# Four instead of five groups of projections for the resting tokens, and an earlier start of two sparse jobs

## The chip, the cores and the metric

The kernel runs on one core of a Trainium2 chip. The metric is the device time of one execution in microseconds, given as the median over several runs.

## The reference

Two layers of a transformer trunk over 256 tokens of width 1024. In each layer one product with a wide matrix gives all projections at once; three kinds of attention work on them, and gates merge their outputs:

```python
fq, fk, fv, ff, sq, sk, sv, dq, dk, dv, iq, ik, iw, g = split_cols(x @ w_in)
# widths:   384 384 384 6  320 320 320  320 64 64  512 64 8  3072
o_fox = fox_attention(fq, fk, fv, log_sigmoid(ff))          # 6 heads, softmax with decay
o_sb  = stick_breaking_attention(sq, sk, sv)                # 5 heads
o_dsa = dsa_attention(rope(dq), rope(dk), dv, rope(iq), rope(ik), iw)   # 5 heads, one k and v
merged = sum(sigmoid(g_i) * (o_i @ w_up_i))
x = layer_norm(alpha * x + merged @ w_out)
x = layer_norm(alpha * x + squared_relu(x @ w_ff_in) @ w_ff_out + gated embedding)
```

(Written here in short; batch, biases and blocks are left out.) The sparse attention (dsa) has an indexer: eight heads of scores `relu(iq . ik)`, weighted with `iw` and summed, pick the 64 keys of a query that its softmax may see. Each head has 64 columns.

## The kernel before

Every float32 value that enters a matmul is held as a high part (a cast by ACT, line 159) and a low part (DVE's subtraction, line 160), made by `split`; a product is three matmuls, high by high, high by low and low by high (`mm3`, line 174). Weights come in units through five buffers each for the raw load (`wr`, line 106), the high part (`wh`) and the low part (`wl`).

The projections are made in two ways. In `xstat` the tokens rest in TensorE and the weights' columns move: a group of up to 512 columns takes two PSUM banks (`pg`, of which there are four in turn), one per tile of 128 tokens, and goes through the eight blocks of 128 inputs in four units of two. A unit is 12 matmuls, six for each token tile, a group 48. Its output has tokens on the partitions, as the values, the gates and the projections that are rotated (`do_rope`, lines 497 to 501 on DVE and an addition on POOL, lines 504 and 506) want it. In `wstat` the weights rest and 256 tokens move; the queries and keys of the fox heads (`fox`, 768 columns, three banks) and of the stick-breaking heads (`sb`, 640 columns, three banks, lines 557 to 560) come that way. When a group ends, its `done` reads the banks; a bank is free for the next group when its last reader is through.

The order is written by hand. `PRODUCTS` names the groups in turn: fv, fox, iq1, iq2, dsa, sb, sv, and then the gates g1 to g5 of 512 columns each. `JOBS` names the attention jobs in turn, each with the number of steps to wait before the next may start: fox0, fox2, fox4 and sb0, sb2, sb4 are pairs of heads (sb4 is the fifth stick-breaking head alone), idxT, idx0 and idx1 the indexer, dsaT transposes, and dsa0, dsa1 and dsa3 sparse heads (one, two and two). The main loop goes by steps. In each step every job in flight goes on to its next yield, the next job starts if its projections are made and the wait is over, and units of projections are issued until 550 columns are reached. After the last unit come at most two units of the up-projections (`up`, 12 matmuls of 512 columns) as filling. Behind the loop, ACT makes the sigmoids of the gates (line 1043, after a load of another function table), and the up-projections go on with sigmoids between them.

A pair of softmax heads goes: scores on TensorE (line 181) into two banks `ps` of four; a reduction with the mask on DVE (line 771), exponentials on ACT (line 774), a reciprocal and a scale on DVE (lines 776 and 779); three transposes per head on TensorE (line 194); the split of the transposed probabilities `t3k` (ACT line 159, DVE line 160); the values, six matmuls (line 174). A stick-breaking job has its own sums (lines 878 to 882), additions (884 and 885), exponential (886), a mask on POOL (841), cast (889) and low part (890) before its values.

Of the kernel before, what the change touches and what calls it, by code (L numbers as in the profile page):

```python
# [10 lines left out]
F32 = mybir.dt.float32  # L11
# [19 lines left out]
PRODUCTS = ['fv', 'fox', 'iq1', 'iq2', 'dsa', 'sb', 'sv', 'g1', 'g2', 'g3', 'g4', 'g5']  # L31
JOBS = [('decay', 4), ('fox0', 2), ('fox2', 2), ('fox4', 1), ('idxT', 1), ('idx0', 3), ('idx1', 0), ('dsaT', 2), ('sb0', 2), ('sb2', 2), ('dsa0', 0), ('sb4', 2), ('dsa1', 1), ('dsa3', 4)]
# [20 lines left out]
def hybrid_trunk(ctx, tc, x, p, w_in, b_forget, w_up_fox, w_up_sb, w_up_dsa, w_out,  # L53
# [29 lines left out]
    def rope_parts(nh):  # L83

        if nh == 1:
            ab = act.tile([P, 2 * HD], F32, tag="t05", name=nm("t05"), bufs=2)
            return [ab[:, i * HD:(i + 1) * HD].rearrange("p (h d) -> p h d", d=HD) for i in range(2)]
        return [t15(F32)[:, :nh * HD].rearrange("p (h d) -> p h d", d=HD) for _ in range(2)]
# [22 lines left out]
    def wrows(w, l, k0, nk, c0, n):  # L111
        return [(ALLP, w[l, k0 * P:(k0 + nk) * P, c0:c0 + n].rearrange("(k p) n -> p k n", p=P))]
# [376 lines left out]
    for l in range(L):  # L489
# [3 lines left out]
        def do_rope(t, src, nh, dst, dup=1):  # L493

            s3 = src.rearrange("p (h d) -> p h d", d=HD)
            a, b = rope_parts(nh)
# [6 lines left out]
            if dup == 1:  # L503
                nc.gpsimd.tensor_add(dst.rearrange("p (h d) -> p h d", d=HD), a, b)
            else:
                nc.gpsimd.tensor_add(dst.rearrange("p (h d) -> p h d", d=HD),
                                     a.to_broadcast([P, dup, HD]), b.to_broadcast([P, dup, HD]))
# [127 lines left out]
        def idx_T():  # L635
            q = ps()
            for t in range(2):
                nc.tensor.transpose(q[:, t * P:(t + 1) * P], rnk[t][:, 0:128], ident)
# [71 lines left out]
        def dsa_T():  # L710
            q = ps()
            for t in range(2):
                nc.tensor.transpose(q[:, t * P:(t + 1) * P], rnk[t][:, 128:256], ident)
# [266 lines left out]
        def chain(*gs):  # L980
# [15 lines left out]
        jobs = {"decay": (("fv",), lambda: decay()), "idxT": (("iq1", "iq2"), idx_T),  # L996
                "idx0": (("iq1", "iq2"), lambda: idx_scores(0)),
                "idx1": (("iq1", "iq2"), lambda: idx_scores(1)),
                "dsaT": (("dsa", "sv"), dsa_T)}
# [229 lines left out]
```

## Time and profile before

| | |
|---|---|
| median of 3 runs | 863.86 us (863.65 to 865.48) |
| the profiled execution | 863.92 us, span 862.2 us, granted clock 0.998 |
| TensorE busy | 850.3 us, 99%, 4691 matmuls |
| DVE busy | 641.5 us, 74%, 1143 instructions |
| ACT busy | 471.3 us, 55%, 753 instructions |
| POOL busy | 65.8 us, 8% |
| DMA | 154.46 MB, 179 GB/s |

The profile's span begins with the first instruction; 1.7 us of the execution's time lie around it. A timeline row gives the start, the busy time of the row's instructions together, engine, line, operation, output and inputs, and in square brackets the idle time before it and who ended it. Matmuls overlap, so that the time of one is read from start to start. The rows below are of layer 1; layer 2 follows in the second half of the span.

### The profile page before, as it was taken

The numbers are of one execution on the slowest core, as the hardware profiler recorded it, in microseconds if no ns is written. First come the engines' busy times: TensorE is split into PE (matmuls) and PEld (weight loads), VectorE is DVE, ScalarE is ACT, GpSimd is POOL, SyncE is SP. The second block draws the span as 40 slices with busy tenths as digits, with TensorE's granted clock in tenths as the row PEclk, the third lists the DMA queues.
The fourth block names the chain that finished last, engine by engine and source line by source line (L and its number), as shares of the span: only waits on it lengthen the run. The fifth ranks groups of instructions, "written<-read, shape, count | busy, mean of one in ns | idle before, by whom it ended". The sixth has DMA issues, their size and how long they took to land.

```text
span 862.2 us, 12952 instructions
## 1 busy us (share of the span) xinstructions
PE 850.3 (99%) x4691; PEld 732.9 (85%) x4691; DVE 641.5 (74%) x1143; ACT 471.3 (55%) x753; POOL 65.8 (8%) x136
## 2 busy tenths in 40 slices
PE   9999999999999999999999999999999999999996
PEld 7999988878888888888889998888788888888885
DVE  5679997779867666666866899967898776666666
ACT  5556657694455454444545566667834544444440
POOL 1012010100011000000100211001001100000100
PEclk9999999999999999999999999999999999999999
DMA  8754665626666666666645557555274766666741
GB/s 265 226 145 132 204 194 171 169 76 205 206 221 190 192 188 193 192 192 205 210 128 156 145 162 226 155 169 171 89 232 153 233 192 187 189 193 194 232 134 50
DMA packets 80385, 154.46 MB, mean 179 GB/s; under 512 B 10305, under 2 KB 26049, under 8 KB 80321
## 3 DMA queue, kind: packets, MB, share of 16 engines
q1 hardware_dynamic: 78720, 149.17, 56.0%
q0 software_dynamic: 1600, 4.46, 1.8%
q8 instruction: 37, 0.61, 0.3%
q14 instruction: 28, 0.22, 0.1%
HBM read 152.30 MB, written 1.05 MB: 178 GB/s over the span
## 4 chain that ended last, share of the span: by engine, by line
PE 85%; issue 6%; DVE 4%; ACT 3%; DMA 1%; POOL 0%; DVEq 0%; SPq 0%; POOLq 0%
PE pg L174 46%; PE ps L1112 14%; PE ps L1116 7%; PE pg L239 4%; PE ps L181 2%; PE pg L557 2%; PE pg L246 2%; PE pg L559 2%; PE pg L560 2%; PE ps L194 1%; DVE wl L160 1%; PE ps L174 1%; PE pg L373 1%; ACT t2k L1043 1%; DMA wr<-in_w_in_dram 1%
## 5 line engine op out<-in xcount | busy, mean ns | idle before, releaser
L160 DVE TENSOR_TENSOR wl<-wr,wh 128x1024 fp32r<-128x1024 f32 (+4 forms) x295 | 333.6, 1143 | 160.1 <-ACT wh L159 157.7
L159 ACT CAST wh<-wr 128x1024 fp32r<-128x1024 f32 (+4 forms) x295 | 288.3, 984 | 286.7 <-PE pg L174 99.8
L174 PE MATMUL pg<-wh,t16k 128*128 128x512 f32 (+4 forms) x784 | 227.6, 365 | 0.1
L174 PE MATMUL pg<-wh,t2k 128*128 128x512 f32 x528 | 165.9, 390 | 0.0
L174 PEld LDWEIGHTS pg<-wh,t16k 128*128 128x128 f32 x784 | 142.9, 188 | 20.7 <-DVE t2k L167 0.7
L174 PE MATMUL pg<-wl,t16k 128*128 128x512 f32 (+4 forms) x392 | 142.0, 362 | 0.0
L1112 PE MATMUL ps<-t16k,wh 128*128 128x512 f32 x512 | 127.8, 391 | 0.0
L174 PEld LDWEIGHTS pg<-wh,t2k 128*128 128x128 f32 x528 | 99.2, 188 | 20.3
L1112 PEld LDWEIGHTS ps<-t16k,wh 128*128 128x128 f32 x512 | 93.1, 189 | 17.3
L174 PE MATMUL pg<-wl,t2k 128*128 128x512 f32 x264 | 102.9, 390 | 0.0
L174 PEld LDWEIGHTS pg<-wl,t16k 128*128 128x128 f32 x392 | 73.7, 188 | 8.5 <-DVE wl L160 0.2
L1116 PEld LDWEIGHTS ps<-t16k,wl 128*128 128x128 f32 x512 | 69.8, 190 | 5.0
L1116 PE MATMUL ps<-t16k,wl 128*128 128x256 f32 x512 | 71.4, 282 | 0.0
L174 PEld LDWEIGHTS pg<-wl,t2k 128*128 128x128 f32 x264 | 49.6, 188 | 9.7
L557 PE MATMUL pg<-t16k,wh 128*128 128x256 f32 x176 | 50.5, 287 | 0.4 <-DVE t16k L160 0.4
L560 PE MATMUL pg<-t16k,wl 128*128 128x256 f32 x176 | 49.8, 283 | 0.0
L559 PE MATMUL pg<-t16k,wh 128*128 128x256 f32 x176 | 49.7, 283 | 0.0
L174 PE MATMUL pg<-wh,t1k 128*128 128x512 f32 x112 | 37.4, 398 | 0.0
L557 PEld LDWEIGHTS pg<-t16k,wh 128*128 128x128 f32 x176 | 33.6, 191 | 0.9 <-issue 0.8
L559 PEld LDWEIGHTS pg<-t16k,wh 128*128 128x128 f32 x176 | 33.7, 191 | 0.0
L560 PEld LDWEIGHTS pg<-t16k,wl 128*128 128x128 f32 x176 | 33.7, 191 | 0.0
L774 ACT ACTIVATE t3k<-t3k,small 128x128 f32<-128x128 f32 (+1 forms) x44 | 19.7, 449 | 14.7 <-DVE small L771 14.7
(211 smaller groups left out, 1002.1 us busy)
## 6 DMA issues: line engine op xcount, KB each, us to landing
wr<-in_w_ff_in_dram SPq DMA_DIRECT2D x64, 512.0 KB, 4.3
wr<-in_w_ff_out_dram SPq DMA_DIRECT2D x64, 512.0 KB, 4.0
wr<-in_w_in_dram SPq DMA_DIRECT2D x46, 512.0 KB, 4.3
wr<-in_w_in_dram SPq DMA_DIRECT2D x32, 384.0 KB, 3.8
wr<-in_w_out_dram SPq DMA_DIRECT2D x16, 512.0 KB, 3.8
wr<-in_w_ple_gate_dram SPq DMA_DIRECT2D x16, 512.0 KB, 4.4
wr<-in_w_in_dram SPq DMA_DIRECT2D x16, 256.0 KB, 3.2
wr<-in_w_in_dram SPq DMA_DIRECT2D x8, 390.0 KB, 4.2
```

What stands on the lines that cost most here:

```text
L159: a = nc.scalar.copy(hi, src)
L160: b = nc.vector.tensor_sub(lo, src, hi.bitcast(F32))
L174: nc.tensor.matmul(o, l, r, start=start and i == 0, stop=stop and i == 2, skip_group_check=skip)
L181: nc.tensor.matmul(o, a[i == 2], b[i == 1], start=start and i == 0, stop=stop and i == 2)
L239: nc.tensor.matmul(o[t][:, :n], tok(aT, u * nk + kk, t)[0], wt[i][kk], start=u + kk + i == 0, stop=False)
L246: nc.tensor.matmul(o[t][:, :n], tok(aT, kb, t)[1], units[kb // nk][0][kb % nk], start=False, stop=kb == nkb - 1)
L557: nc.tensor.matmul(oi, hi, rh, start=kb == 0 and i % 2 == 0, stop=False, skip_group_check=True)
L559: nc.tensor.matmul(oi, hi, rl, start=False, stop=False, skip_group_check=True)
L560: nc.tensor.matmul(oi, lo, rh, start=False, stop=kb == KB - 1, skip_group_check=True)
L774: nc.scalar.activation(pr[:, i, sl], pr[:, i, sl], AF.Exp, bias=mn[:, t:t + 1], scale=-1.0, accum_out=mn[:, 2 + t:3 + t])
L1112: nc.tensor.matmul(pz[i], wt[0][:, kk, i * P:(i + 1) * P], x1_both[:, 2 * u + kk, :], start=u + kk == 0, stop=False, skip_group_check=True)
L1116: nc.tensor.matmul(pz[i][:, 0:T], wt[1][:, kk, i * P:(i + 1) * P], x1T[0][:, 2 * u + kk, :], start=False, stop=2 * u + kk == KB - 1, skip_ ...
```

## The change

The 1742 columns that go through `xstat` are cut anew. Before: fv 390, iq1 320, iq2 264, dsa 384, sv 384. Now: fv 390, iq 512 (all eight indexer queries), ix 392 (three sparse query heads, the sparse key and value, the indexer key and weights; loaded by two transfers a unit, of 320 and of 72 columns), sv 448 (the stick-breaking values and the first two sparse query heads). The ropes follow: iq two of four heads, ix one of two heads (both keys, each written twice) and one of three, sv one of two. In `JOBS` the step between sb4 and dsa1 goes from 2 to 1.

With a group fewer, the steps that issue projections go from 28 to 26 a layer. Counted from the last of them, dsa1 and dsa3 start one unit of 12 matmuls earlier, sb0, sb2 and dsa0 one unit later. The number of loads of weights in these groups is 16 a layer before and now. `PE` has 4691 matmuls before, and 48 a layer fewer now.

The core of the diff:

```diff
-PRODUCTS = ['fv', 'fox', 'iq1', 'iq2', 'dsa', 'sb', 'sv', 'g1', 'g2', 'g3', 'g4', 'g5']
-JOBS = [('decay', 4), ('fox0', 2), ('fox2', 2), ('fox4', 1), ('idxT', 1), ('idx0', 3), ('idx1', 0), ('dsaT', 2), ('sb0', 2), ('sb2', 2), ('dsa0', 0), ('sb4', 2), ('dsa1', 1), ('dsa3', 4)]
+PRODUCTS = ['fv', 'fox', 'iq', 'ix', 'sb', 'sv', 'g1', 'g2', 'g3', 'g4', 'g5']
+JOBS = [('decay', 4), ('fox0', 2), ('fox2', 2), ('fox4', 1), ('idxT', 1), ('idx0', 3), ('idx1', 0), ('dsaT', 2), ('sb0', 2), ('sb2', 2), ('dsa0', 0), ('sb4', 1), ('dsa1', 1), ('dsa3', 4)]
...
-        def c2_done(t, o):
-            do_rope(t, o[:, 192:256], 1, rnk[t][:, 0:128], dup=2)
-            nc.vector.tensor_copy(iw[t], o[:, 256:264])
-            do_rope(t, o[:, 0:192], 3, rnq[t][:, 320:512])
-
-        def c1_done(t, o):
-            do_rope(t, o[:, 0:320], 5, rnq[t][:, 0:320])
+        def iq_done(t, o):
+            for c in (0, 256):
+                do_rope(t, heads(o[:, c:c + 256]), 4, heads(rnq[t][:, c:c + 256]))
...
-        def c4_done(t, o):
-            split(o[:, 320:384], vh[:, t, 768:832], vl[:, t, 768:832])
-            do_rope(t, o[:, 256:320], 1, rnk[t][:, 128:256], dup=2)
-            do_rope(t, o[:, 0:256], 4, rnd[t][:, 64:320])
-            nc.gpsimd.tensor_copy(rnd[t][:, 320:384], rnk[t][:, 128:192])
+        def ix_done(t, o):
+
+            split(o[:, 256:320], vh[:, t, 768:832], vl[:, t, 768:832])
+
+            do_rope(t, o[:, 192:448].rearrange("p (h c) -> p h c", c=2 * HD)[:, :, 0:HD], 2,
+                    rnk[t].rearrange("p (h c) -> p h c", c=2 * HD), dup=2)
+            nc.vector.tensor_copy(iw[t], o[:, 384:392])
+            do_rope(t, heads(o[:, 0:192]), 3, heads(rnd[t][:, 128:320]))
+            nc.gpsimd.tensor_copy(rnd[t][:, 320:384], rnk[t][:, 0:64])
             for v in (vh, vl):
                 nc.gpsimd.tensor_copy(v[:, t, 832:896], v[:, t, 768:832])
 
-        def c3_done(t, o):
+        def sv_done(t, o):
             split(o[:, 0:320], vh[:, t, 384:704], vl[:, t, 384:704])
-            do_rope(t, o[:, 320:384], 1, rnd[t][:, 0:64])
+            do_rope(t, heads(o[:, 320:448]), 2, heads(rnd[t][:, 0:128]))
...
-            "iq2": (KB, 264, lambda: xstat(xT, w_in, l, O_IQ + 320, 264, c2_done)),
-            "iq1": (KB, 320, lambda: xstat(xT, w_in, l, O_IQ, 320, c1_done)),
-            "dsa": (KB, 384, lambda: xstat(xT, w_in, l, O_DQ + 64, 384, c4_done)),
-            "sv": (KB, 384, lambda: xstat(xT, w_in, l, O_SV, 384, c3_done)),
+            "iq": (KB, 512, lambda: xstat(xT, w_in, l, O_IQ, 512, iq_done)),
+            "ix": (KB, 392, lambda: xstat(xT, w_in, l, [(O_DQ + 128, 320), (O_IK, 72)], 392, ix_done)),
+            "sv": (KB, 448, lambda: xstat(xT, w_in, l, O_SV, 448, sv_done)),
```

The rest of the diff lets `wrows` take a list of column ranges, lets `do_rope` write a head twice for two heads at once, and changes the names in the jobs' conditions. Behind the changed lines the line numbers are eight to eleven higher.

The order on the engines changes at three places that matter below. First, DVE where the first stick-breaking unit waits for a bank, in layer 1. `ps_1038` and `ps_1039` are the score banks of a pair of fox heads (`mfox` is their mask), `pg_948` is the bank of the first token tile of the group dsa. Before:

```order
L771 ISA t3k_1037,small_1145<-ps_1039,mfox 128x256
L771 ISA small_1145 128x1
L776 RECIPROCAL small_1056<-small_1056 128x2
L160 TENSOR_TENSOR t16k_288<-pg_948,t16k_288 128x64
L779 TENSOR_SCALAR t3k_1037<-t3k_1037,small_1056 128x128
L779 TENSOR_SCALAR t3k_1037<-t3k_1037,small_1056 128x256
L497 TENSOR_TENSOR t_214_1084<-pg_948,rope 128x64
L499 TENSOR_TENSOR t_214_1084<-pg_948,rope 128x32
L501 TENSOR_TENSOR t_214_1084<-pg_948,rope 128x32
L497 TENSOR_TENSOR t_215_1089<-pg_948,rope 128x256
L499 TENSOR_TENSOR t_216_1090<-pg_948,rope 128x4x32
L501 TENSOR_TENSOR t_216_1090<-pg_948,rope 128x4x32
```

Now, where `ps_876` and `ps_877` are score banks of fox heads and `pg_827` is the bank of the first token tile of ix:

```order
L782 ISA small_894 128x1
L787 RECIPROCAL small_894<-small_894 128x2
L790 TENSOR_SCALAR t3k_875<-t3k_875,small_894 128x128
L790 TENSOR_SCALAR t3k_875<-t3k_875,small_894 128x256
L168 TENSOR_TENSOR wl_1107<-wr_1103,wh_1106 128x640
L168 TENSOR_TENSOR t16k_288<-pg_827,t16k_288 128x64
L504 TENSOR_TENSOR t_188_942<-pg_827,rope 128x128
L506 TENSOR_TENSOR t_188_942<-pg_827,rope 128x2x32
L508 TENSOR_TENSOR t_188_942<-pg_827,rope 128x2x32
L707 COPY small_337<-pg_827 128x8
L504 TENSOR_TENSOR t_189_948<-pg_827,rope 128x192
L506 TENSOR_TENSOR t_190_949<-pg_827,rope 128x3x32
```

The ropes of the first tile stood behind the reductions of both heads. Now one head's reduction, reciprocal and scales are ahead, a weight subtraction stands between, and the other head's reductions come behind the ropes of both tiles.

Second, DVE around the low part of the fifth stick-breaking head. `t3k_2075` (before) and `t3k_2019` (now) are that low part, `wl_` low parts of weights, the rows with `mt_` reductions of a sparse head. Before:

```order
L160 TENSOR_TENSOR wl_2242<-wr_2239,wh_2241 128x1024
L884 TENSOR_TENSOR t3k_1971<-t3k_1971,ps_2063 128x128
L885 TENSOR_TENSOR t3k_1971<-t3k_1971,ps_2062 128x256
L890 TENSOR_TENSOR t3k_2051<-t3k_1826,t3k_2050 128x768
L160 TENSOR_TENSOR t3k_2055<-ps_2056,t3k_2054 128x384
L890 TENSOR_TENSOR t3k_2075<-t3k_1971,t3k_2074 128x384
L160 TENSOR_TENSOR wl_2281<-wr_2277,wh_2280 128x1024
L160 TENSOR_TENSOR wl_2316<-wr_2312,wh_2315 128x1024
L746 TENSOR_TENSOR t1k_364<-ps_2120,t1k_364 64x256
L746 TENSOR_TENSOR t1k_363<-ps_2129,t1k_363 64x256
L771 ISA t3k_2138,small_2153<-ps_2139,mt_1404 128x128
```

Now:

```order
L168 TENSOR_TENSOR t1k_360<-ps_1970,t1k_359 64x256
L896 TENSOR_TENSOR t3k_1911<-t3k_1911,ps_2006 128x256
L895 TENSOR_TENSOR t3k_1911<-t3k_1911,ps_2007 128x128
L901 TENSOR_TENSOR t3k_1995<-t3k_1766,t3k_1994 128x768
L168 TENSOR_TENSOR t3k_1999<-ps_2000,t3k_1998 128x384
L168 TENSOR_TENSOR wl_2255<-wr_2251,wh_2254 128x1024
L901 TENSOR_TENSOR t3k_2019<-t3k_1911,t3k_2018 128x384
L782 ISA t3k_2022,small_2037<-ps_2023,mt_1392 128x128
L782 ISA small_2037 128x1
L782 ISA t3k_2022,small_2037<-ps_2023,mt_1718 128x256
```

Before, two weight subtractions and two low parts of head outputs stood between the low part and the next reductions. Now one weight subtraction has moved ahead of the low part, and the reductions follow directly behind it.

Third, ACT where the gates' sigmoids begin. `t3k` rows are casts of transposed probabilities; the last of them (`ps_2344` before, `ps_2245` now) is that of the last sparse head. Before:

```order
L159 CAST wh_2415<-wr_2413 128x1024
L1043 ACT_TABLE_LOAD
L1043 ACTIVATE t2k_323<-t2k_323,small_2361 128x512
L159 CAST t3k_2261<-ps_2298 128x384
L159 CAST t3k_2304<-ps_2306 128x384
L1043 ACTIVATE t2k_325<-t2k_325,small_2361 128x512
L1043 ACTIVATE t2k_1802<-t2k_1802,small_2361 128x512
L1043 ACTIVATE t2k_1804<-t2k_1804,small_2361 128x512
L1043 ACTIVATE t2k_2096<-t2k_2096,small_2361 128x512
L1043 ACTIVATE t2k_2098<-t2k_2098,small_2361 128x512
L159 CAST t1k_365<-ps_2333 64x256
L159 CAST t3k_2304<-ps_2344 128x384
```

Now the same stretch, from the exponentials of the last sparse pair to the two gate copies:

```order
L785 ACTIVATE t3k_2109,small_2124<-t3k_2109,small_2124 128x128
L785 ACTIVATE t3k_2109,small_2124<-t3k_2109,small_2124 128x256
L785 ACTIVATE t3k_2109,small_2191<-t3k_2109,small_2191 128x128
L785 ACTIVATE t3k_2109,small_2191<-t3k_2109,small_2191 128x256
L167 CAST wh_2319<-wr_2315 128x1024
L1053 ACT_TABLE_LOAD
L1053 ACTIVATE t2k_323<-t2k_323,small_2283 128x512
L526 COPY t2k_2168<-pg_2045 128x512
L526 COPY t2k_2170<-pg_2046 128x512
L167 CAST t1k_361<-ps_2172 64x256
L167 CAST t3k_2183<-ps_2185 128x384
```

and, some rows on, to the last cast:

```order
L167 CAST t3k_2205<-ps_2207 128x384
L1053 ACTIVATE t2k_325<-t2k_325,small_2283 128x512
L1053 ACTIVATE t2k_1689<-t2k_1689,small_2283 128x512
L1053 ACTIVATE t2k_1691<-t2k_1691,small_2283 128x512
L1053 ACTIVATE t2k_1966<-t2k_1966,small_2283 128x512
L1053 ACTIVATE t2k_1968<-t2k_1968,small_2283 128x512
L167 CAST t1k_365<-ps_2234 64x256
L167 CAST wh_2337<-wr_2335 128x1024
L167 CAST t1k_365<-ps_2234 64x256
L167 CAST t3k_2205<-ps_2245 128x384
```

The two gate copies and all the exponentials were ahead of the table load and further apart. Now the exponentials of the last sparse pair stand directly ahead of a weight cast and the table load, and the last cast still follows five sigmoids, with a second weight cast ahead of it.

## Rows read from the trace of the kernel before

**Rows 1.** The page: busy times, and the costliest group of projection matmuls.

```profile
PE 850.3 (99%) x4691; PEld 732.9 (85%) x4691; DVE 641.5 (74%) x1143; ACT 471.3 (55%) x753; POOL 65.8 (8%) x136
...
L174 PE MATMUL pg<-wh,t16k 128*128 128x512 f32 (+4 forms) x784 | 227.6, 365 | 0.1
```

**Rows 2.** The list of waits of TensorE: total us, times, longest.

```profile
PE ps L174 <- ACT t3k L159: 1.6, 2, 0.8
```

**Rows 3.** Timeline, TensorE and DVE, 76.9 to 77.9 us, layer 1.

```profile
76.93 0.41 DVE L497 TENSOR_TENSOR t<-pg,rope 128x256 f32<-128x256 f32 x1
...
77.42 0.27 PE L194 MATMUL ps<-ident,t3k 128*128 128x128 f32 x1
77.46 0.28 DVE L501 TENSOR_TENSOR t<-pg,rope 128x128 f32<-128x128 f32 x1
...
77.88 0.35 PE L557 MATMUL pg<-t16k,wh 128*128 128x256 f32 x1 [0.19 <-DVE t16k L160]
```

**Rows 4.** Timeline, DVE and TensorE, 97 to 98.5 us: the group sv.

```profile
97.15 0.66 DVE L167 SCALAR_TENSOR_TENSOR t2k<-pg,t2k 128x512 fp32r<-128x512 f32 x1
...
97.49 0.83 PE L174 MATMUL pg<-wh,t16k 128*128 128x384 f32 x2
...
98.16 0.34 PE L174 MATMUL pg<-wl,t16k 128*128 128x384 f32 x1
```

**Rows 5.** Timeline of TensorE, 154 to 186 us: the end of the attention, layer 1.

```profile
154.03 1.19 PE L174 MATMUL ps<-t3k,t16k 128*128 128x512 f32 x6
...
162.68 1.71 PE L174 MATMUL ps<-t3k,t16k 128*128 128x256 f32 x12
...
183.94 0.63 PE L174 MATMUL pg<-wh,t1k 128*128 128x512 f32 x2
185.39 0.51 PE L174 MATMUL ps<-t3k,t16k 128*128 128x512 f32 x1 [0.82 <-ACT t3k L159]
```

**Rows 6.** Timeline of ACT, the same stretch.

```profile
154.23 1.05 ACT L159 CAST wh<-wr 128x1024 fp32r<-128x1024 f32 x1 [1.67 <-PE pg L174]
...
177.80 1.06 ACT L159 CAST wh<-wr 128x1024 fp32r<-128x1024 f32 x1
178.88 1.28 ACT L1043 ACT_TABLE_LOAD   x1
...
180.80 0.84 ACT L159 CAST t3k<-ps 128x384 fp32r<-128x384 f32 x2
181.53 3.18 ACT L1043 ACTIVATE t2k<-t2k,small 128x512 f32<-128x512 f32 x5
...
184.86 0.48 ACT L159 CAST t3k<-ps 128x384 fp32r<-128x384 f32 x1
```

**Rows 7.** Timeline of DVE, the same stretch.

```profile
162.99 0.56 DVE L890 TENSOR_TENSOR t3k<-t3k,t3k 128x384 fp32r<-128x384 f32 x1 [0.38 <-ACT t3k L889]
...
167.12 0.29 DVE L771 CUSTOM_DVE_ANT_0 t3k<-ps,mt 128x128 f32<-128x128 f32 x1
...
167.69 0.28 DVE L771 CUSTOM_DVE_ANT_0 t3k<-ps,mt 128x128 f32<-128x128 f32 x1
...
168.74 0.55 DVE L779 TENSOR_SCALAR t3k<-t3k,small 128x128 f32<-128x128 f32 x2
...
170.36 1.23 DVE L160 TENSOR_TENSOR wl<-wr,wh 128x1024 fp32r<-128x1024 f32 x1 [0.19 <-ACT wh L159]
```

**Rows 8.** Timeline of TensorE: first and last matmuls counted, of 264 and 512 columns.

```profile
59.81 0.28 PE L174 MATMUL pg<-wl,t16k 128*128 128x264 f32 x1
...
61.27 0.28 PE L174 MATMUL pg<-wl,t16k 128*128 128x264 f32 x1
...
168.28 0.39 PE L174 MATMUL pg<-wl,t16k 128*128 128x512 f32 x1
...
170.32 0.39 PE L174 MATMUL pg<-wl,t16k 128*128 128x512 f32 x1
```

**Rows 9.** Timeline of TensorE, 195 to 196.5 us: the up-projections.

```profile
195.72 0.38 PE L194 MATMUL ps<-ident,t2k 128*128 128x128 f32 x2
196.11 0.50 PE L174 MATMUL pg<-wl,t1k 128*128 128x512 f32 x1
```

More of the change, by code (lines that the diff above doesn't have):

```diff
@@ L81, in t15, with rope_parts @@
         return act.tile([P, 384], dt, tag="t15", name=nm("t15"), bufs=T15)
[L83 to L87, printed above, removed]
+    def rope_parts(nh, own):
+        if own:
+            ab = act.tile([P, 4 * HD], F32, tag="t05", name=nm("t05"), bufs=1)
+            return [ab[:, i * 2 * HD:(i + 1) * 2 * HD].rearrange("p (h d) -> p h d", d=HD) for i in range(2)]
         return [t15(F32)[:, :nh * HD].rearrange("p (h d) -> p h d", d=HD) for _ in range(2)]
@@ L111, in wrows @@
     def wrows(w, l, k0, nk, c0, n):
-        return [(ALLP, w[l, k0 * P:(k0 + nk) * P, c0:c0 + n].rearrange("(k p) n -> p k n", p=P))]
+        rows = w[l, k0 * P:(k0 + nk) * P, :].rearrange("(k p) n -> p k n", p=P)
+        if isinstance(c0, int):
+            return [((ALLP, slice(0, nk), slice(0, n)), rows[:, :, c0:c0 + n])]
+        srcs, d = [], 0
+        for c, m in c0:
+            srcs.append(((ALLP, slice(0, nk), slice(d, d + m)), rows[:, :, c:c + m]))
+            d += m
+        return srcs
     nc.scalar.preload_act_table_set("natural_log_exp_and_others")
@@ L491, in hybrid_trunk, with do_rope @@
         vh, vl = vhl[:, 0], vhl[:, 1]
-        def do_rope(t, src, nh, dst, dup=1):
-            s3 = src.rearrange("p (h d) -> p h d", d=HD)
-            a, b = rope_parts(nh)
+        def do_rope(t, s3, nh, dst, dup=1):
+            a, b = rope_parts(nh, dup > 1)
             nc.vector.tensor_mul(a, s3, rope[:, t, None, :].to_broadcast([P, nh, HD]))
@@ L503, in do_rope, with heads @@
             if dup == 1:
-                nc.gpsimd.tensor_add(dst.rearrange("p (h d) -> p h d", d=HD), a, b)
+                nc.gpsimd.tensor_add(dst, a, b)
             else:
-                nc.gpsimd.tensor_add(dst.rearrange("p (h d) -> p h d", d=HD),
-                                     a.to_broadcast([P, dup, HD]), b.to_broadcast([P, dup, HD]))
+                nc.gpsimd.tensor_add(dst.rearrange("p h (c d) -> p h c d", d=HD),
+                                     a[:, :, None, :].to_broadcast([P, nh, dup, HD]),
+                                     b[:, :, None, :].to_broadcast([P, nh, dup, HD]))
+        def heads(ap):
+            return ap.rearrange("p (h d) -> p h d", d=HD)
         gates = {}
@@ L637, in idx_T @@
             for t in range(2):
-                nc.tensor.transpose(q[:, t * P:(t + 1) * P], rnk[t][:, 0:128], ident)
+                nc.tensor.transpose(q[:, t * P:(t + 1) * P], rnk[t][:, 128:256], ident)
             split(q[:, 0:256], *ikT)
@@ L712, in dsa_T @@
             for t in range(2):
-                nc.tensor.transpose(q[:, t * P:(t + 1) * P], rnk[t][:, 128:256], ident)
+                nc.tensor.transpose(q[:, t * P:(t + 1) * P], rnk[t][:, 0:128], ident)
             for t in range(2):
@@ L994, in hybrid_trunk @@
             products[f"g{c}"] = (KB, 512, lambda c=c: gate(c))
[L996 to L999, printed above, removed]
+        jobs = {"decay": (("fv",), lambda: decay()), "idxT": (("iq", "ix"), idx_T),
+                "idx0": (("iq", "ix"), lambda: idx_scores(0)),
+                "idx1": (("iq", "ix"), lambda: idx_scores(1)),
+                "dsaT": (("ix", "sv"), dsa_T)}
         for h in (0, 2, 4):
@@ L1004, in hybrid_trunk @@
         for hs in ((0,), (1, 2), (3, 4)):
-            jobs[f"dsa{hs[0]}"] = (("dsa", "sv", "iq1", "iq2"), lambda hs=hs: dsa_heads(hs))
+            jobs[f"dsa{hs[0]}"] = (("ix", "sv", "iq"), lambda hs=hs: dsa_heads(hs))
         emitted, finished, flight, wait, ups, n_up = set(), set(), [], 0, up(), 0
```

## The prediction

> **What bounds the kernel now.** I read the page's summary first. TensorE is busy for 850.3 of 862.2 us and the others far less [rows 1], so a change gains where it takes work off TensorE or shortens one of its waits, and loses where it makes a wait. Next came the wait between the projection groups: the groups' matmuls have 0.1 us of idle time before them in all their 784 instructions [rows 1], so weights are never late there, and the casts, subtractions and transfers that the regrouping saves lie beside other work. Third came TensorE's own timeline, start to start, since its busy time hides waits inside a merged group. It shows four places per layer: 77.42 us [rows 3], 97.49 us [rows 4], 162.68 us and 183.94 us [rows 5]. After these I read ACT and DVE in the same stretch, from 154 to 186 us [rows 6, 7]. The second layer repeats the first: the wait for the last cast stands twice in the list of waits, 1.6 us in all, the longest 0.8 [rows 2].
>
> All is summed against the profiled execution, 863.92 us; the median of the runs is 863.86, the same for every purpose here. What a measurement can tell from no change is about 0.2%, or 1.7 us: below 862.1 is faster, above 865.6 is slower.
>
> **The change, part by part.** *Fewer, longer matmuls.* Twelve matmuls of 264 columns take 1.46 us, from 59.81 to 61.27, or 0.1217 each; nine of 512 take 2.04, from 168.28 to 170.32, or 0.2267 each [rows 8]. The line through the two is 0.0099 us for the matmul and 0.000423 us for a column. A group issues 48 matmuls of one width, and the columns are the same before and after (264 + 320 + 384 + 384 and 512 + 392 + 448, both 1352), so one group fewer saves 48 x 0.0099 = 0.48 us a layer, **1.0 us** in two. Bounds: a start is read to 0.01 us, and the slope of the line may be that of the granted clock's upper level, 2.4 GHz (the clock is 0.998 of it over the span): then the excess is 0.2267 - 0.2133 = 13 ns on 512 columns and 0.1217 - 0.1100 = 12 ns on 264. So 0.8 to 1.3.
>
> The Trainium skill, page "TensorE: Matmul & The Clock Gate", section "Wait — 56ns, not 53.3ns?", says that a warm matmul costs a fixed 2.5 ns or so beyond its columns. By that rule 96 matmuls fewer at equal columns are worth only an estimated 0.24 us; the rows, measured with this kernel's fp32r operands and a weight load for each matmul, show four to five times as much, and the sum goes by them.
>
> *Casts, subtractions, transfers.* Four units of weights a layer drop a cast on ACT and a subtraction on DVE; the number of loads stays at 16 a layer, since one group now takes two transfers a unit. Cover: the weights' lead, seen in the 0.1 us above [rows 1]. If that cover were gone, each unit would show its own subtraction, about 1 us. I take nothing.
>
> *The rope's bank.* At 77.42 us TensorE wants its third bank for the stick-breaking projections, which is that of the preceding group's first token tile; the last rope instruction reading it begins at 77.46 and lasts 0.28 [rows 3]. From 77.42 to 77.88 one transpose of 128 columns is done, 0.06 by the line above, so 0.40 is lost. In the new order one head's reductions, reciprocal and scales leave DVE before the first tile's ropes and the other head's reductions follow behind the second tile's. The tile's last matmul ends six matmuls, 6 x 0.176 = 1.06 us, before the group's end; a rope of four heads takes 0.81 us (76.93 to 77.74 [rows 3]), and the tile now has one of two heads and one of three, under 1.6 us, so the bank is free about 0.6 us after the group's end. TensorE wants it after 12 matmuls of 256 columns, 12 x 0.118 = 1.4 us. The margin of 0.8 us is what DVE may be behind. I take the whole wait as gone, **0.4 us a layer** (bounds 0 and 0.45).
>
> *The bank of the last group.* At 97.49 two matmuls of 384 columns take 0.67 us where 0.35 would do; the second is held by the split of the stick-breaking queries, 97.15 plus 0.66 [rows 4]. With 448 columns the first tile's six matmuls of the unit last 6 x 0.0267 = 0.16 us longer, so the bank is wanted that much later, and the split stands slightly earlier on DVE. I take **0.2 us a layer** (bounds 0 and 0.32). Both together: 1.2 us in two layers.
>
> *The sparse jobs one step on.* This is where something is lost. I count from 154.03 us, where the values of the first pair of stick-breaking heads start [rows 5], and call it 0; the new order is followed with the durations of the rows, start to start.
> - DVE and ACT first. In the new order a weight cast and its subtraction stand ahead of the fifth stick-breaking head's cast and low part. The cast ends at about 9.15, an estimate from ACT's new order (the middle pair's exponential can begin at 5.2, when its sums are added up, and another exponential, three casts and POOL's mask come before the weight cast); then come the subtraction 1.23 and the low part 0.56, to 10.9 [rows 7]. Now the first reductions of the sparse pair (heads 1 and 2) run: a head takes 0.57 us (167.12 to 167.69 [rows 7]), so two end at 12.05. Behind them: a weight subtraction 1.23, the scales of two heads 0.55 each, and four smaller ones (two reciprocals and two low parts, each shorter than the 0.56 of the row with 384 columns; I take 0.28 on the mean), to 15.5. Then the reductions of the last pair, to 16.6, and its exponentials on ACT, to 17.5.
> - ACT from there to the last pair's final cast: two weight casts 1.08 and 1.03, the table load with one sigmoid 1.92 (178.88 to 180.80), three casts of transposed probabilities at 0.37 (two in 0.73 to 181.53), five sigmoids 3.2, the cast itself 0.48 [rows 6], and six smaller instructions, two gate copies (512 columns like a sigmoid) and four casts of 256 columns (shorter than those of 384), for which I take 1.9: 10.7, so it ends at 28.2.
> - TensorE. Before, it reached this point at 184.40 (two matmuls after 183.94 [rows 5]), or 30.37. Of that 0.26 was waiting. The new order has 16 matmuls of 512 columns fewer on the way (12 of the projections are issued ahead, 4 of the up-projection behind), 3.63 us. It has 0.95 of waits that I find on the way: 0.25 for a bank of the pair's first scores, 0.2 for the fifth head's low part, and 0.5 for banks that the reductions free at 12.05. So it arrives at 27.4 and waits 0.8, and 0.3 more for the low part.
> Waits in this tail are then 0.95 + 1.1 = 2.05, against 1.37 before (0.26 in the 12 matmuls from 162.68 and 1.11 from 183.94 on [rows 5]): 0.68 more. One wait goes: from 195.72 to 196.11 two transposes take 0.39 where 0.13 would do by the line, and the next matmul is 0.50 long instead of 0.39 [rows 9], waiting for a low part of weights. In the new order that subtraction stands further ahead on DVE, by some 3 us, so 0.33 is taken off. The tail costs **0.35 us a layer, 0.7 in all**; bounds below with the rivals.
>
> The sum: -1.0 - 1.2 + 0.7 = -1.5, so 863.92 - 1.5 = **862.4 us**.
>
> **The rivals.** *First, the tail does not wait at the end.* ACT's queue of 10.7 us needs to be only 0.8 shorter, or the reductions earlier by that, and the last cast is ready when TensorE arrives. For it: the rows' casts and sigmoids run back to back, and DVE's list of 3.4 us between the two reductions has pieces that ACT may have finished early. Against: the queues are in program order, and ACT is already the releaser of this wait, 0.8 us in each layer [rows 2]. Then 1.1 a layer goes: 862.4 - 2.2 = 860.2.
>
> *Second, slower: the weight cast ahead of the fifth head's cast is held.* It needs a weight buffer which TensorE frees at about 7.3 by my count, and starts at 8.1, a margin of 0.8 us. Whatever it is late beyond that moves the low part, both reductions, the exponentials and the final cast one for one, and TensorE waits at the end. The time is over the upper bound from 1.6 us a layer on; a hold of 1.8 gives 862.4 + 3.6 = 866.0. For it: ACT stands 1.67 us for just such a buffer at the start of this stretch [rows 6]. Against: there it costs TensorE nothing, and the hold would have to be longer than that, beyond the margin, in both layers.
>
> *Third, the 12 ns do not go with the number of matmuls* but with something that long ones have as well, such as a weight load that the columns do not cover: 13 ns at 512 columns against 12 at 264 [rows 8] leave room for a part that grows. If only a quarter of the 48 x 0.0099 is saved, the first term is 0.25 instead of 1.0, and the time is 863.2. The page named above speaks for this case.
>
> *Fourth, the jobs move but no wait does*, because DVE is as far behind at both banks and the tail's waits only change places: only 1.0 is left, 862.9.
>
> **How the numbers follow.** The forecast, with its own spread from 861.2 to 864.0 (terms of 0.8 to 1.3, of 0 to 1.5, and the end's wait by half a microsecond a layer either way): 0.52. The first rival 0.25, the second 0.13, the third 0.06, the fourth 0.04. Faster: the first rival and a third of the forecast, 0.25 + 0.18 = 0.43. Slower: the second, 0.13. Same: the rest, 0.44. The range from 860.0 to 865.8 leaves out the lower part of the first rival (0.08) and most of the second (0.10). Both signs hold much, so the likeliest's own range above stands beside it.
>
> **What would show it.** TensorE's instructions fall by 96, and its busy time by about 1 us. The wait at the rope's bank is gone from the list of waits. The bank of the last group is waited for by 0.1 instead of 0.3. In the tail, about 28 us after the first pair's values, TensorE still waits for ACT's cast, by about 0.8 us, with the reductions of the last pair beginning near 15.5. The first rival shows as no such wait, the second as an idle ACT ahead of a weight cast, released by TensorE. I am wrong if a new wait stands between 98 and 154 us, where TensorE now has none, or in the layer's output projection.

## The result, and the profile after

The changed kernel is slower: 870.10 us median of six runs against 864.56 of the kernel before, ratio 1.0059 (95% interval 1.0044 to 1.0073). One of the six runs took 2994.38 us and is left out of the ratio; the median of the other five is 869.43. Run a second time, word for word, it took 868.96 against 865.00, ratio 1.0047 (1.0030 to 1.0064). The forecast was 862.4 us, with a range that ended at 865.8: the time moved to the other side.

The page of the changed kernel, where [rows 1] stood:

```profile
PE 852.3 (98%) x4595; PEld 728.5 (84%) x4595; DVE 637.4 (73%) x1123; ACT 468.7 (54%) x745; POOL 66.6 (8%) x132
...
L182 PE MATMUL pg<-wh,t16k 128*128 128x512 f32 (+3 forms) x720 | 223.4, 383 | 0.1
```

TensorE has 96 matmuls fewer. That it is busy 2.0 us longer says little: in a second profile of each kernel it is 851.4 us before and 851.3 now. The groups' matmuls still have 0.1 us of idle time before them, so weights are in time. The list of waits, where [rows 2] stood:

```profile
PE ps L182 <- ACT t3k L167: 2.4, 2, 1.2
...
PE pg L247 <- ACT t16k L167: 0.5, 2, 0.3
PE ps L189 <- DVE small L782: 0.5, 2, 0.2
```

The wait for the last cast has grown from 0.8 to 1.2 us a layer, and two waits are new: for DVE's reductions before scores, and for ACT's cast in the step behind layer normalization. The wait for the rope's bank stood in the list of the kernel before, and is gone from it now:

```profile
PE pg L557 <- DVE t16k L160: 0.4, 2, 0.2
```

A table by stages shows where the 5 us lie. A stage ends where, in TensorE's timeline, the first matmul of the next starts: the first projection of 390 columns, the first MLP matmul (line 1112, now 1122). The first stage is counted from TensorE's first matmul, 1.26 us behind the span's start, and the last one to the start of its last matmul. All in us:

| profile of | first matmul to first projection | layer 1, projections to MLP | layer 1, MLP to next projections | layer 2, projections to MLP | layer 2, MLP to last matmul |
|---|---|---|---|---|---|
| before | 18.73 | 222.77 | 203.81 | 220.59 | 187.08 |
| the change | 20.87 | 224.40 | 203.85 | 221.89 | 187.08 |
| before, again | 20.33 | 222.85 | 203.81 | 220.28 | 187.08 |
| the change, again | 18.71 | 224.34 | 206.03 | 221.96 | 187.08 |

Two layers of attention cost 1.6 and 1.3 us more in the first pair of profiles, 1.5 and 1.7 in the second. The start differs by 2.1 us one way and 1.6 the other, so it is not the change's. This matters for every median below: a median mixes runs with a short and with a long start, so that differences of a microsecond between medians are read from the stages as well. And 2.2 us stand once in the MLP of the changed kernel, which the change doesn't touch either. The experiments take these apart.

The attention's end in layer 1, TensorE, where [rows 5] stood:

```profile
158.16 1.19 PE L182 MATMUL ps<-t3k,t16k 128*128 128x512 f32 x6
...
161.28 0.61 PE L182 MATMUL pg<-wh,t16k 128*128 128x512 f32 x2
162.00 0.52 PE L202 MATMUL ps<-ident,t3k 128*128 128x128 f32 x3
...
164.09 1.41 PE L189 MATMUL ps<-t1k,t2k 64*128 64x128 f32 x12
...
170.19 0.32 PE L189 MATMUL ps<-t1k,t2k 64*128 64x128 f32 x1
170.74 0.32 PE L189 MATMUL ps<-t1k,t1k 64*128 64x128 f32 x1 [0.23 <-DVE small L782]
...
185.88 0.39 PE L182 MATMUL pg<-wh,t1k 128*128 128x512 f32 x1
187.47 1.70 PE L182 MATMUL ps<-t3k,t16k 128*128 128x512 f32 x6 [1.21 <-ACT t3k L167]
189.01 0.39 PE L182 MATMUL pg<-wh,t1k 128*128 128x512 f32 x1
```

Counted from 158.16 (the values of the first pair): two matmuls from 161.28 should end at 161.73, and the transposes come at 162.00, 0.27 late. The 12 scores from 164.09 take 1.33 us (the next row starts at 165.42), where a stall-free dozen takes 0.9, and come 0.2 late. The second scores lose 0.55 less 0.06 at 170.19, and came 0.2 late. The last values start 1.59 us behind a matmul that takes 0.23, 1.36 late, and their six matmuls take 1.54 instead of 1.04. ACT, where [rows 6] stood:

```profile
174.54 0.41 ACT L785 ACTIVATE t3k<-t3k,small 128x128 f32<-128x128 f32 x1 [2.26 <-DVE small L782]
...
182.15 3.17 ACT L1053 ACTIVATE t2k<-t2k,small 128x512 f32<-128x512 f32 x5
...
186.94 0.48 ACT L167 CAST t3k<-ps 128x384 fp32r<-128x384 f32 x1
```

ACT has nothing to do for 2.26 us ahead of the last pair's exponentials, and then works without a pause up to the last cast at 186.94. DVE, where [rows 7] stood:

```profile
159.93 1.46 DVE L168 TENSOR_TENSOR wl<-wr,wh 128x1024 fp32r<-128x1024 f32 x1
...
168.79 0.55 DVE L901 TENSOR_TENSOR t3k<-t3k,t3k 128x384 fp32r<-128x384 f32 x1
169.49 0.29 DVE L782 CUSTOM_DVE_ANT_0 t3k<-ps,mt 128x128 f32<-128x128 f32 x1
...
170.60 1.22 DVE L168 TENSOR_TENSOR wl<-wr,wh 128x1024 fp32r<-128x1024 f32 x1
...
174.21 0.29 DVE L782 CUSTOM_DVE_ANT_0 t3k<-ps,mt 128x128 f32<-128x128 f32 x1
```

A weight subtraction of 1.46 us, where others take 1.2, stands at 159.93 ahead of the steps that TensorE waits for at 162.00. The low part of the fifth head ends near 169.3, the first pair of reductions near 170.6, and the last ones begin at 174.21.

### The profile page after: what moved, and what is told of

Same layout as the page of the kernel before. It is cut to its first block, busy times and chain, and to the rows that moved or that the text cites. A ratio compares the mean times of both kernels' runs of the same rounds, so it can differ in the third digit from the quotient of the medians.

```text
span 867.3 us, 12716 instructions
## 1 busy us (share of the span) xinstructions
PE 852.3 (98%) x4595; PEld 728.5 (84%) x4595; DVE 637.4 (73%) x1123; ACT 468.7 (54%) x745; POOL 66.6 (8%) x132
## 4 chain that ended last, share of the span: by engine, by line
PE 91%; ACT 4%; DVE 2%; issue 1%; DMA 1%; POOL 0%; SPq 0%; DVEq 0%; ACTq 0%
PE pg L182 49%; PE ps L1122 14%; PE ps L1126 7%; PE pg L247 4%; PE pg L568 3%; PE pg L570 2%; PE pg L571 2%; PE ps L189 2%; PE pg L254 2%; PE ps L202 1%; PE pg L381 1%; ACT wh L167 1%; PE ps L182 1%; ACT t2k L1053 1%; DMA w<-in_w_ple_dram 1%
## 5 line engine op out<-in xcount | busy, mean ns | idle before, releaser
L168 DVE TENSOR_TENSOR wl<-wr,wh 128x1024 fp32r<-128x1024 f32 (+5 forms) x287 | 332.6, 1168 | 169.1 <-ACT wh L167 165.1
L167 ACT CAST wh<-wr 128x1024 fp32r<-128x1024 f32 (+5 forms) x287 | 287.2, 1007 | 295.0 <-PE pg L182 117.9
L182 PE MATMUL pg<-wh,t16k 128*128 128x512 f32 (+3 forms) x720 | 223.4, 383 | 0.1
L182 PEld LDWEIGHTS pg<-wh,t16k 128*128 128x128 f32 x720 | 134.4, 188 | 24.9 <-ACT t16k L167 1.0
L182 PE MATMUL pg<-wl,t16k 128*128 128x512 f32 (+3 forms) x360 | 136.8, 380 | 0.0
L182 PEld LDWEIGHTS pg<-wl,t16k 128*128 128x128 f32 x360 | 67.6, 188 | 10.2 <-DVE wl L168 0.2
```

Source lines behind the costliest of these rows:

```text
L167: a = nc.scalar.copy(hi, src)
L168: b = nc.vector.tensor_sub(lo, src, hi.bitcast(F32))
L182: nc.tensor.matmul(o, l, r, start=start and i == 0, stop=stop and i == 2, skip_group_check=skip)
```

## The experiments

**The two parts alone, and both kernels again.** The grouping alone is the changed kernel with

```diff
-('sb4', 1)
+('sb4', 2)
```

and the job's step alone is the kernel before with the opposite edit. Expected of the first:

> The four groups with the old step of 2 between sb4 and dsa1. Three theories for the 5 us: (A) the earlier sparse jobs cost it in the tail of the attention, (B) the regrouping itself costs it by moving everything else against the tail, (C) the first 2.1 us, lost before any projection starts, are chance of the first loads and belong to no part of the change. A: the waits of TensorE around the last cast go back to about 1.3 us a layer, the stretch from the first projection to the up-projections is 1.2 us or more shorter per layer than with the whole change, and the time is 863 +- 1 us (865 if the start slips too). B: at least 866 us without a slip of the start.

of the second:

> The kernel before with the step of sb4 at 1 instead of 2, nothing else. A: slower than before by about 2 to 4 us (1 to 2 us a layer in the tail). B: within 1 us of before.

and of the two kernels word for word:

> The changed kernel once more, word for word. C: the first matmuls of the projections start anywhere between 20 and 22 us, and the time of this run is 867 to 870 us. If the slip belongs to the changed kernel they start near 22 us again and the time is 869 to 870.

> The kernel before once more, word for word: ratio 1.000 within 0.002. C: its projections may start later than 19.9 us in this profile. If the slip belongs to the changed kernel, they start at 19.9 us again.

Measured: the grouping alone 868.33 (ratio 1.0043, 1.0027 to 1.0058), the step alone 867.43 (1.0029, 1.0020 to 1.0039), the change again 868.96, before again 864.97 (1.0000, 0.9988 to 1.0012). The start was 18.71 us in the change again and 20.33 in before again: C holds, it is chance, in both kernels. The step alone costs 2.4 us, as A said. By stages the step alone needs 224.06 and 221.62 us, 1.3 and 1.0 more than before. But it does not lose them where A looked, at the last cast: that wait has left its list, and two others stand there.

```profile
PE pg L174 <- DVE t1k L160: 0.6, 2, 0.3
PE pg L239 <- ACT t16k L159: 0.5, 2, 0.3
```

The first is for the low part of an attention output in the up-projections, the second for the cast behind layer normalization. From the first matmul of line 932, with which the later up-projections begin, to the MLP, the step alone takes 56.86 us in each layer against 55.76 and 55.99 before; ahead of line 932 it loses only 0.2.

The grouping alone took 223.40 and 220.98, only 0.6 and 0.4 more than before; but its MLP stage took 207.52, 3.7 more. The wait for the last cast has left its list too, and two waits for DVE, for the low part of a stick-breaking head and for a sparse head's scale, have come:

```profile
PE ps L182 <- DVE t3k L901: 0.9, 2, 0.5
PE ps L202 <- DVE t3k L790: 0.9, 2, 0.4
```

So by its median (over 866) B seemed right, and by its stages, 1.0 and 0.9 us shorter than those of the whole change, more nearly A, which had asked for 1.2.

**The load of the embedding input.** The 2.2 and 3.7 us stand at one place, TensorE's transposes of the second layer's embedding input (`pn`). Its load in the kernel before, and in the changed kernel's second profile (time of the issue, who waited, landing):

```profile
L100 SPq DMA_DIRECT2D pn<-in_p_dram x1: 378/378/378, 414.3 to 414.3; - x1
...
DMA to landing us min/median/max: 4.3/4.3/4.3
```

```profile
L100 SPq DMA_DIRECT2D pn<-in_p_dram x1: 887/887/887, 415.5 to 415.5; - x1
...
DMA to landing us min/median/max: 7.3/7.3/7.3
```

In the kernel before, TensorE's weight load that reads it starts 4.7 us after the issue, in the other kernels up to 5.0. It landed after 4.2 to 4.8 us in all four profiles of the old grouping and in the first of the change, after 7.0 to 7.3 in three of the four of the new. In the grouping alone the wait drew something behind it:

```profile
424.55 0.92 PE L346 MATMUL ps<-ident,pn 128*128 128x128 f32 x4 [1.91 <-DMA pn<-in_p_dram]
...
426.12 1.05 PE L182 MATMUL pg<-wh,t2k 128*128 128x512 f32 x2
426.98 0.63 PE L182 MATMUL pg<-wl,t2k 128*128 128x512 f32 x1
```

After 1.91 us of idle time two matmuls of 512 columns take 0.86 us instead of 0.45: the granted clock was at the lower of its two levels, 1.2 GHz, for about 3 us (0.54 on the mean from 424.5 to 427.5), which is the rest of the 3.7. This profile is of the slowest of the six runs of the grouping alone. To take the wait away both kernels issue this load one MLP block earlier:

```diff
+            if c == NC - 2 and l < L - 1:
+                p1 = load_p(l + 1)
             if c == NC - 1 and l < L - 1:
-                p1 = load_p(l + 1)
```

> The changed kernel with the second layer's embedding input loaded one block of the MLP earlier. (C2) In two of three profiles of regrouped kernels TensorE waited 1.9 to 2.0 us for this load at the layer boundary, its landing 7.1 to 7.3 us after issue instead of 4.2 to 4.8, in no profile of the other grouping: if that chance wait makes the rest between the 3.0 us that the stages show and the 4.0 to 5.5 us of the medians, the wait never shows here and the median is 867.5 to 868.3 us, 3.0 us above the same edit of the kernel before. (D) If the rest is elsewhere, the time stays at 869 or more.

> The same earlier load in the kernel before. C2: unchanged within 0.5 us of 865.0, as its load was in time in each profile; D says the same.

Measured: the change 867.01 (1.0028, 1.0015 to 1.0041), before 864.70 (1.0002, 0.9990 to 1.0013). Both kernels bear out C2's cause, 2 us of the change's loss are this load, and none of before's time. The median is 0.5 us under C2's range and 2.3 us above before, not 3.0; the stages of the two profiles differ by 2.9. The same with the grouping alone:

> The four groups with the old step for sb4 and with the earlier load. Stage by stage it was 1.1 us over before (223.4 and 221.0 us a layer from the first projections to the MLP, against 222.8 and 220.6), the rest of its 3.3 us being the late load and the lower clock behind it. With the load early: 865.8 us, 1.0 over before with the same load.

864.90 (0.9997, 0.9984 to 1.0009): 3.4 us less than without, 0.9 less than forecast, and no difference to before by the medians. By stages it takes 223.27 and 220.97 us, against 223.05 and 220.39 of before with the same load: 0.8 us more. With the load early, then, the grouping gains nothing (a loss of 0.2 by medians, of 0.8 by stages), and the step on top of it costs 2.1, by medians (867.01 against 864.90) and by stages.

Why the load lands late with the new grouping is not settled. Its issue stands 0.43 us behind that of a load of weights in the four profiles of the new grouping, and 0.71 us in three of the old. But of those four it landed in time in one, the first profile of the change (after 4.6 us), and in the step alone it stands 0.44 us behind and landed in time as well (after 4.8 us): a short distance alone does not make it late.

**The last cast.** Is it ACT's queue that TensorE waits for in the tail? The cast of the last sparse head's transposed probabilities goes to DVE:

```diff
-                split(q[:, 0:384], pT[0][:, i, :], pT[1][:, i, :])
+                if n == 14 and i == 1:
+                    nc.vector.tensor_copy(pT[0][:, i, :], q[:, 0:384])
+                    nc.vector.tensor_sub(pT[1][:, i, :], q[:, 0:384], pT[0][:, i, :].bitcast(F32))
+                else:
+                    split(q[:, 0:384], pT[0][:, i, :], pT[1][:, i, :])
```

> The changed kernel with the cast of the last sparse head's transposed probabilities on DVE instead of ACT, where it stands behind five sigmoids. (A) If ACT's queue is what TensorE waits for before the last values, 1.37 us of the 1.74 a layer go and some 0.4 stays for the low part: 2.5 us less, 866.5 us, and the wait for ACT's cast leaves the list of waits. (E) If another late input takes its place (the low part behind another low part on DVE, or weights), less than 1 us is gained.

> The same cast on DVE in the kernel before. A: 1.11 us a layer waits there, about 0.9 of it goes: 863.2 us, 1.8 us less than before, which would beat both. E: within 0.7 us of before.

Measured: 868.11 in the changed kernel (1.0043, 1.0027 to 1.0059), within the noise of 868.96, as E said, and 867.00 in the kernel before (1.0023, 1.0011 to 1.0034), slower than either forecast: by stages 223.66 and 221.43 us, and TensorE waits for the next cast (0.7 us a layer) and for the low part (0.4). A fell in this form. By stages the changed kernel's layers are at 224.41 and 221.95, as before the edit. The list of waits of the edited changed kernel:

```profile
PE pg L182 <- ACT t1k L167: 2.0, 2, 1.0
```

The old wait is gone and TensorE waits 1.0 us a layer a little later for the next cast in ACT's queue, that of the attention's output. One cast taken out of a full queue passes the wait on.

**A shorter queue on ACT.** So the queue itself is shortened: the two copies of the last gate group out of PSUM go to DVE (with the earlier load in all kernels).

```diff
-                nc.scalar.copy(g, o)
+                (nc.vector.tensor_copy if c == 5 else nc.scalar.copy)(g, o)
```

> The changed kernel with the earlier load of the embedding input, and with the two copies of the last gate group out of PSUM on DVE instead of ACT. (F) If ACT's whole queue from the last exponentials on is what holds TensorE in the tail (moving one cast only passed the wait to the next cast), a queue that is 1.0 us shorter a layer gives back 0.8 to 1.0 us a layer: about 865.2 us against 867.0 without it, and the wait for the last cast falls from 1.2 to about 0.3 us. (G) If DVE or the matmul order holds it, less than 0.3 us a layer.

> The same two edits in the kernel before. F: its wait for the last cast is 0.8 us a layer, so up to 0.8 a layer is gained, unless the copies on DVE hold up the last pair's scales: 863.0 to 864.0 us. G: 864.7 unchanged.

> regroup_p with the two gate copies on DVE. F: 0.3 to 0.9 us a layer less, 864.0 to 865.2 us. G: 865.8.

Measured: the change 866.61 (1.0027, 1.0016 to 1.0039), 0.4 less; the grouping alone 865.70 (1.0004, 0.9992 to 1.0016), 0.8 more; the kernel before **862.69** (0.9973, 0.9960 to 0.9985), 2.0 less, **faster than both kernels**. The stages of the profiles, free of the start, in us:

| with the load early | median | start | layer 1, projections to MLP | layer 2, projections to MLP |
|---|---|---|---|---|
| before | 864.70 | 20.44 | 223.05 | 220.39 |
| grouping alone | 864.90 | 21.25 | 223.27 | 220.97 |
| the change | 867.01 | 18.67 | 224.41 | 221.96 |
| before, copies on DVE | 862.69 | 21.12 | 222.67 | 219.31 |
| grouping alone, copies on DVE | 865.70 | 21.02 | 222.91 | 220.59 |
| the change, copies on DVE | 866.61 | 18.73 | 224.11 | 221.69 |

By stages the copies gain 1.5, 0.7 and 0.6 us in the three kernels; the grouping alone gains 0.4 a layer, at the lower end of F, though its median rose. TensorE at the last values of the changed kernel with this edit:

```profile
184.04 0.39 PE L182 MATMUL pg<-wh,t1k 128*128 128x512 f32 x1
184.48 0.50 PE L182 MATMUL ps<-t3k,t16k 128*128 128x512 f32 x1
185.28 1.08 PE L182 MATMUL ps<-t3k,t16k 128*128 128x512 f32 x5 [0.29 <-DVE t3k L168]
```

In the kernel before, the 1.1 us of waiting at the last values are gone, and its list of waits names them no longer. That gives 1.1 us in layer 2, but only 0.4 in layer 1, where a new wait stands in the output projection's second half:

```profile
PE pg L239 <- DVE wl L160: 0.7, 1, 0.7
```

In the changed kernel the cast is now in time to 0.2 us, and the second matmul waits 0.29 us for DVE's low part. (The bracket counts from the modelled end of the matmul before; from start to start 0.57 us are lost, which is called "with the release" below.) The rest is given back behind, where the stretch from line 943 to the MLP is 0.4 us longer in each layer. F holds for the kernel before, and for a third of its size in the changed one: there DVE is nearly as late as ACT.

**The width of a matmul.** In the changed kernel's timeline of TensorE, widths are read as in [rows 8]: between the starts of the two rows of 392 columns lie 15 matmuls, and 15 between those of 448:

```profile
69.32 0.34 PE L182 MATMUL pg<-wl,t16k 128*128 128x392 f32 x1
...
72.00 0.34 PE L182 MATMUL pg<-wl,t16k 128*128 128x392 f32 x1
```

```profile
101.81 0.36 PE L182 MATMUL pg<-wl,t16k 128*128 128x448 f32 x1
...
104.91 0.37 PE L182 MATMUL pg<-wl,t16k 128*128 128x448 f32 x1
```

A matmul of 392 columns takes 2.68 / 15 = 0.179 us, as the line said within 0.003; one of 448 takes 3.10 / 15 = 0.2067 instead of 0.1995. Whether the layout of the weights makes it or the width:

```diff
+        w = 512 if n == 448 else n
-        hi = wp.tile([P, nk, n], ...)
+        hi = wp.tile([P, nk, w], ...)[:, :, 0:n]
```

> The changed kernel with the earlier load, the weights of the 448-column group held at a pitch of 512 columns in their tiles. In the profile of the changed kernel a matmul of 448 columns takes 0.2067 us, 20 ns beyond its columns, where 384 and 512 columns have 13. (H) If the pitch of the moving operand's rows makes it: 0.200. (I) If the width makes it: 0.207 again.

and the group at 456 and 480 columns:

> The same group at 456 columns; the 8 columns more are computed and not used. The line through 264 and 512 columns gives 0.2029 us. H: 0.203 or 0.210 by its own pitch. I, as a property of 448 alone: 0.203. I, as a range of widths between 392 and 512: 0.210.

> The same group at 480 columns, 32 of them not used. The line gives 0.2131 us. I as a range of widths: 0.220.

The timelines of TensorE with the other pitch, at 456 and at 480 columns, 15, 18 and 18 matmuls from the first row to the last, one run each:

```profile
101.87 0.36 PE L182 MATMUL pg<-wl,t16k 128*128 128x448 f32 x1
...
104.97 0.37 PE L182 MATMUL pg<-wl,t16k 128*128 128x448 f32 x1
```

```profile
99.69 0.36 PE L182 MATMUL pg<-wl,t16k 128*128 128x456 f32 x1
...
103.41 0.37 PE L182 MATMUL pg<-wl,t16k 128*128 128x456 f32 x1
```

```profile
100.02 0.38 PE L182 MATMUL pg<-wl,t16k 128*128 128x480 f32 x1
...
103.96 0.38 PE L182 MATMUL pg<-wl,t16k 128*128 128x480 f32 x1
```

Each takes 0.2067, 0.2067 and 0.2189 us. H falls. 456 columns cost what 448 do, halfway between the 0.203 and 0.210 forecast, and 480 stands 19 ns over its columns where 512 has 13. The widths tried between 392 and 512 cost 4 to 7 ns more than the line. The three runs took 869.06, 866.90 and 868.04 us, too few to compare; at 480 columns layer 1 is 0.5 us longer from the projections to the MLP than at 448 or 456, as 48 such matmuls would make it. What makes the width dear is open.

## Why the prediction was wrong, point by point

The step that failed is the sum of the waits in the attention's tail: 0.68 us a layer more than before was forecast, 2.2 were read. That error alone turns the sign, from -1.5 us to +1.5. Three more add to it: the matmuls saved are worth a third, the output projection's gain was a loss, and the late load was in no term.

**Fewer, longer matmuls: 1.0 forecast, 0.3 measured.** The widths that [rows 8] does not show, 15 matmuls from row to row in the kernel before:

```profile
49.81 0.31 PE L174 MATMUL pg<-wl,t16k 128*128 128x320 f32 x1
...
52.01 0.31 PE L174 MATMUL pg<-wl,t16k 128*128 128x320 f32 x1
```

```profile
100.83 0.33 PE L174 MATMUL pg<-wl,t16k 128*128 128x384 f32 x1
...
103.43 0.33 PE L174 MATMUL pg<-wl,t16k 128*128 128x384 f32 x1
```

Four of the old matmuls cost 0.1467 (320 columns) + 0.1217 (264) + 2 x 0.1733 (384) = 0.6150, and the three that take their place 0.2267 (512) + 0.179 + 0.2067 = 0.6124 or less: 48 x 0.003 = 0.13 to 0.17 us a layer. The term was mis-sized by drawing a straight line over widths that no row showed; its lower bound of 0.8 was too high as well. By luck the sum of two layers is near the 0.24 us that the prediction estimated by the rule of the Trainium skill, page "TensorE: Matmul & The Clock Gate", section "Wait — 56ns, not 53.3ns?". The trace does not agree with the rule itself: no width here is nearer than 11 ns to its columns.

**The rope's bank and the last group's bank: right.** Where [rows 3] lost 0.40, the unit after the group now runs through:

```profile
73.43 0.49 PE L202 MATMUL ps<-ident,t3k 128*128 128x128 f32 x3
73.67 0.36 PE L568 MATMUL pg<-t16k,wh 128*128 128x256 f32 x1
```

and its third bank, 12 matmuls on, is taken without a stall. In the first unit of sv, where [rows 4] lost 0.3, 12 matmuls of 448 columns take 2.47 us (95.81 to 98.28), 0.206 each. 0.4 and 0.3 us a layer were gained, 1.4 in all against 1.2 forecast.

**The sparse jobs one step on: right in its chain, too small in its sum, and this decided the sign.** Counted from the first pair's values, forecast and measured: the first reductions end at 12.05 and 12.4; the last begin at 15.5 and 16.05; the last exponential ends at 17.5 and 18.2; the last cast at 28.2 and 29.3; TensorE arrives at 27.4 and 27.9. Each step was late by a little, and the errors added up in one direction. The waits: 0.27 at the transposes, not foreseen; 0.6 at the first scores against 0.25; 0.14 against 0.2 at the low part; 0.7 at the second scores against 0.5; 1.36 and 0.5 at the last values against 0.8 and 0.3. In all 3.6 us against 2.05, so 2.2 us a layer more than before instead of 0.68. The step makes about half of this: with the load early, the runs with it and without it on the new grouping are 2.1 us apart, 1.1 and 1.0 a layer by stages. The rest comes with the grouping, to which the prediction laid no loss at all: alone it should have gained the 2.2 us of the first two terms, and its new waits for DVE in the tail (0.9 us each in two layers, above) ate up what it gained ahead of them. On the old grouping the step costs about as much, 2.4 us, but behind the last values and not at them, so the place of its loss depends on the grouping. The cast at the last values was put down to ACT's queue; shortening that queue showed DVE's low part almost as late (0.57 with the release, against 0.3 in the sum), and gave back only 0.3 us a layer.

**The later up-projections and the output projection: 0.33 a layer forecast as a gain, 0.1 to 0.5 measured as a loss.** From the first matmul of line 932 (now 943) to the MLP both kernels have the same 258 matmuls; in layer 1 they take 55.76 us before and 56.13 in the changed kernel, 55.82 and 56.11 in the second profiles, in layer 2 55.99 and 56.08, 55.68 and 56.14. The wait of [rows 9] went as forecast. In its place came others, of which the clearest is one that the order, not any edited line, makes. The last transposes ahead of the gated embedding, before and in the changed kernel:

```profile
235.89 0.60 PE L194 MATMUL ps<-ident,x 128*128 128x128 f32 x4
236.25 0.48 PE L246 MATMUL pg<-wh,t16k 128*128 128x512 f32 x1
236.56 0.60 PE L194 MATMUL ps<-ident,x 128*128 128x128 f32 x4
```

```profile
239.62 1.05 PE L202 MATMUL ps<-ident,x 128*128 128x128 f32 x8
240.95 0.73 PE L247 MATMUL pg<-t2k,t16k 128*128 128x512 f32 x2 [0.27 <-ACT t16k L167]
```

Before, matmuls stood between the two groups of transposes and covered ACT's cast. Now eight transposes stand together and the next matmul waits 0.27 us for that cast, 0.5 with the release. The same happened with either part of the change alone; an edit that undoes only this was not tried. It is close to the sign that the prediction gave for being wrong, a new wait in the output projection.

**The load of the embedding input: 2 us, not in the sum at all.** The prediction looked for stages that the change touches. This transfer had landed 0.4 us before it was needed, and the margin fell away without any edit near it.

**The rivals.** The second had the right sign and the wrong place: no cast was held by a buffer beyond its margin. The first, ACT in time at the end, was farthest off. The third was right in its size, 0.25 us left of the first term, though the cause it named was not tested; in the fourth no wait was to move, and several did. The sum of the corrected terms for a layer is -0.15 - 0.4 - 0.3 + 2.2 + 0.3 = 1.65 us (the 0.3 is the output projection's loss on the mean), where the stages show 1.6 for layer 1. With two layers and the load's 2 us that makes 5.3, where the stages of the second profiles show 5.4, and the medians, the one long run left out, 4.0 and 4.9.

## What to carry to other kernels

A chain of several engines whose steps are all taken at their shortest gives a bound from below, not a middle: put the range's weight on its late side. A step of work that is started earlier is worth nothing if the engines that finish it are full; count what each queue holds until the next thing TensorE wants, and shorten the queue (here two copies moved from ACT to DVE, 1.5 us by stages and 2.0 by medians in the kernel before), not the one instruction that is waited for. Look behind the next wait too: in the changed kernel the same two copies gave 0.6 us, since DVE was nearly as late. And list the transfers that land less than half a microsecond before their use anywhere in the program: a change elsewhere can take that margin.

## What the runs showed of the hardware

Matmuls of 448, 456 and 480 columns take 0.2067, 0.2067 and 0.2189 us, 20, 17 and 19 ns beyond their columns at 2.4 GHz, while 384 and 512 columns have 13 ns. The stretch ahead of the first projections, which no edit here touches, took 18.7 to 21.4 us over the profiles, and 18.7 and 20.9 in two of the changed kernel; what makes the difference is not shown. At the layer boundary an idle stretch of about 2 us was followed by about 3 us at the lower clock in one profile (after 1.91 us) and not in two others (after 2.04 and 1.8 us).
